# FOX attention of block 1 by pairs of heads: softmax normalised before the transposes, P V in feature order

## The chip, the cores and the metric

The kernel runs on one core of a Trainium2 chip. The metric is the device time of one execution in microseconds, from the median of several runs. The engines are PE (TensorE), DVE (VectorE), ACT (ScalarE), POOL (GpSimd) and SP (SyncE, which here only issues DMAs). Each takes its instructions strictly in the order in which they stand in its own program, and waits on semaphores of the others.

## The reference

Two transformer layers in float32 on 256 tokens with width 2048. The change lies in the first, a hybrid layer that puts 16 meta tokens ahead of the sequence:

```python
xn = _rms(h, n1)
proj = xn @ w_in
z_rwkv, z_fox, z_gate = jnp.split(proj, (RWKV_COLS, RWKV_COLS + FOX_COLS), axis=-1)
...
y_a = _rwkv7(z_rwkv, w0, w2, a0, a2, g2, k_k, k_a, r_k, gn_w, gn_b)
y_b = _fox(z_fox, q_g, k_g, f_bias)
...
merged = g_a * (y_a @ w_a) + g_b * (y_b @ w_b)
h = h + merged @ w_o
```

`_fox` is softmax attention with a forget gate over 16 heads of 64 features, in blocks of queries (the 16 meta queries' own outputs are dropped at the end):

```python
sc = jnp.einsum('bqhd,bkhd->bhqk', q[:, s:e], k[:, :e]).astype(F32) * ATTN_SCALE
sc = sc + c[:, :, s:e, None] - c[:, :, None, :e]
...
p = jax.nn.softmax(jnp.where(causal, sc, -jnp.inf), axis=-1)
outs.append(jnp.einsum('bhqk,bkhd->bqhd', p.astype(v.dtype), v[:, :, :e]))
```

`_rwkv7` is a linear recurrence over tokens with 16 heads of 64, followed by a group norm. A feed-forward layer, and a second layer with stick-breaking and latent attention, follow unchanged.

## The kernel before

Large products are made of three products of split operands (`mm3`): a weight tile comes by SP into one of three `raw` buffers, ACT casts it to `hi` (L219), DVE subtracts to get `lo` (L220), and PE multiplies hi by hi, hi by lo and lo by hi (all PE products are recorded at L240, the body of `mm`). Names in the profile are tile tags: `g`, `q` and `f` are PSUM banks (four, two and two of them): `g` for projections and gates, `q` for the RWKV work, `f` for FOX.

Block 1 goes through four groups q of four RWKV heads (`rwkv(q)`, a generator that yields between its stages) and four of four FOX heads (`fox(q)`). The loop interleaves them: projections and Gram matrices of RWKV group q, then the group norm of the group before, then the inverse and recurrence of group q, then `fox(q)`, then some of the eight gate products (`gate(n)`, weights w_g, results kept in DRAM as gdr).

One RWKV group is a long serial chain: the Gram matrices gt go through DRAM (hd) into tile hs (tag `hq`); DVE inverts 32x32 blocks by 31 steps of substitution (L573 multiplies, L576 adds; tiles xx and xt, tag `c`, xx loaded by POOL from xinit at L563); the result goes to DRAM (qd) and back (tags `hq` and `qf`); DVE copies and transposes it (L585, L587); small products complete the 64x64 inverses (q<-c,gt and q<-hq,c); a recurrence over five chunks follows (PE q<-sbd,x, DVE L633, PE q<-g_,qf, ACT L636, PE q<-uv,kb and q<-uv,gt, DVE L651); then a group norm (L664 to L679), and `to_units`, which transposes the result to feature order (four PE transposes, L420), copies it by ACT into `ysq` (L422) and writes it to DRAM (ydr0, L423).

A FOX head: POOL builds the bias (L738, L739), PE makes the scores for the two blocks of 128 queries (144 and 272 keys, contraction 64), DVE adds the bias and takes the maximum (L743), ACT exponentiates and sums (L745). PE transposes the unnormalised P: two transposes of the 16 meta keys (L748, L749) and three of 128 keys (L752 to L754). P V is a product with P's transposes as the stationary operand: five products of 64 columns into rows of queries. DVE divides by the sums (L764), and `to_units` transposes a group of four heads to feature order (through `ysf` into DRAM, ydr1).

After the loop the merge runs `for b in (1, 0)`: first y_b (read from ydr1) by w_b, 192 products, each half multiplied by its gate on DVE (L849), then y_a (read from ydr0, L836) by w_a, added to it. Then w_o. SP loads all weights in its own order, among them the reads of ydr.

The tile framework's scheduler sets the order of the instructions on each engine: from priorities, dependences, and the time at which a buffer of a tag's ring comes free. Weight loads are given priority (AHEAD = 300). `tmpf` takes a tile from a ring of five buffers with tag `c`; xx, xt, and most large temporaries of the RWKV group come from it. The group-norm, transposed and recurrent tiles therefore share buffers in the order in which they are made.

Of the kernel before, what the change touches and what calls it, by code (L numbers as in the profile page):

```python
# [17 lines left out]
META = 16  # L18
# [177 lines left out]
def body(tc, a, out):  # L196
# [5 lines left out]
    with ExitStack() as top:  # L202
# [83 lines left out]
        # ================= block 1: attention branches =================  # L286
        xh = T(xp, [128, 16, L], "X0", F32R)
        xl = T(xp, [128, 16, L], "X1", F32R)
        with ExitStack() as ph:
# [12 lines left out]

            def tmpp(shape):
                return T(rp, shape, "p", bufs=4)
# [76 lines left out]
            # forget gate: nc = cumsum(softplus(-(fl + bias)))  # L381
# [33 lines left out]
            def to_units(src, dst, tag):  # L415
                # src natural [128, 2, 256] -> dst [feature, 2, token]
                ps = bank(tag)
                for j in range(2):
                    for t in range(2):
                        P.transpose(ps[:, 256 * j + 128 * t:256 * j + 128 * t + 128], src[:, t, 128 * j:128 * j + 128], ident)  # L420
                ys = T(rp, [128, 512], "ys" + tag)
                S.copy(ys, ps)  # L422
                G.dma_start(dst, ys)  # L423

# [5 lines left out]
            def rwkv(q):  # L430
# [63 lines left out]
                # Gram matrices  # L494
# [25 lines left out]
                # bonus  # L520
# [6 lines left out]
                # natural v, and stacked [U | V]  # L527
# [17 lines left out]
                # natural [b | k]  # L545
# [14 lines left out]
                # inverse of (I - N): 32 x 32 diagonal blocks by substitution  # L560
# [36 lines left out]
                # L_ak V for every chunk  # L597
# [8 lines left out]
                # recurrence over chunks  # L606
# [50 lines left out]
                # group norm, bonus, gate  # L657
# [26 lines left out]
            def fox(q):  # L684
# [30 lines left out]
                vm = T(rp, [16, 256], "vm")  # L715
# [4 lines left out]
                S.copy(vn[:, :, :256], ps.rearrange("p (a b) -> p a b", b=256))  # L720
                ps = bank("f")
                for j in range(2):
                    P.transpose(ps[:16, 128 * j:128 * j + 128], vz[:, j, 0:META], ident)
                S.copy(vm, ps[:16, :256])
                yo = tmpo()
                st = T(rp, [128, 4, 8], "fst")
                for h in range(4):
                    j, er = h // 2, slice(64 * (h % 2), 64 * (h % 2) + 64)
                    hg = 4 * q + h
                    mb = tmpp([128, 416])  # L730
                    sm = tmpp([128, 416])
                    fm = C("fox")
                    rng = (slice(0, 144), slice(144, 416))
                    ps = bank("f")
                    for t in range(2):
                        n = 144 + 128 * t
                        m_ = mb[:, rng[t]]
                        G.tensor_scalar(out=m_, in0=ckb[:, h, :n], scalar1=cq[:, t, hg:hg + 1], scalar2=qs[:, 0, t, h:h + 1], op0=ALU.subtract, op1=ALU.mult)  # L738
                        G.tensor_tensor(out=m_[:, n - 128:], in0=m_[:, n - 128:], in1=fm, op=ALU.add)  # L739
                        mm(ps[:, rng[t]], qn[er, j, 128 * t:128 * t + 128], kn[er, j, :n])  # L740
                    for t in range(2):
                        sidx = 4 * t + h
                        V.tensor_tensor_reduce(out=sm[:, rng[t]], in0=ps[:, rng[t]], in1=mb[:, rng[t]], scale=1.0, scalar=-BIG, op0=ALU.add, op1=ALU.max, accum_out=st[:, 0, sidx:sidx + 1])  # L743
                        V.tensor_scalar(out=st[:, 1, sidx:sidx + 1], in0=st[:, 0, sidx:sidx + 1], scalar1=qs[:, 2, t, h:h + 1], scalar2=None, op0=ALU.mult)  # L744
                        S.activation(sm[:, rng[t]], sm[:, rng[t]], AF.Exp, bias=st[:, 1, sidx:sidx + 1], scale=qs[:, 1, t, h:h + 1], accum_out=st[:, 2, sidx:sidx + 1])  # L745
                    pt, pm = tmpp([128, 3, 128]), tmpp([16, 2, 128])
                    ps = bank("f")
                    P.transpose(ps[:16, 0:128], sm[:, 0:16], ident)  # L748
                    P.transpose(ps[:16, 128:256], sm[:, 144:160], ident)  # L749
                    V.tensor_copy(pm.rearrange("p a b -> p (a b)"), ps[:16, 0:256])  # L750
                    po = bank("f")
                    P.transpose(po[:, 0:128], sm[:, 16:144], ident)  # L752
                    P.transpose(po[:, 128:256], sm[:, 160:288], ident)
                    P.transpose(po[:, 256:384], sm[:, 288:416], ident)  # L754
                    S.copy(pt.rearrange("p a b -> p (a b)"), po[:, 0:384])
                    hs_ = slice(64 * h, 64 * h + 64)
                    for t in range(2):
                        o = po[:, 384 + 64 * t:448 + 64 * t]
                        mm(o, pm[:, t], vm[:, hs_], True, False)
                        mm(o, pt[:, t], vn[:, 0, hs_], False, t == 0)  # L760
                        if t:
                            mm(o, pt[:, 2], vn[:, 1, hs_], False, True)
# [420 lines left out]
```

## Time and profile before

| | |
|---|---|
| median of 3 runs | 2046.07 us (2041.98 to 2047.33) |
| profiled execution, its span | 2038.6 us |
| PE busy | 2010.6 us (99%) |
| DVE, ACT, POOL busy | 1219.6, 953.1, 160.4 us |
| mean DMA rate | 178 GB/s |
| idle stretches of PE over 2 us after the start | 172.6 (3.0 us) and 741.5 (2.5 us) |

The profiled execution is one run of its own; its time is given by the span, from its first to its last instruction. A row of the timeline gives the start, the duration, the engine, the line, the operation, the tile written <- the tiles read, the shape of the stationary operand for PE (rows*columns), the shapes and the count of the instructions that the row joins, and in brackets the idle time before and what ended it. A plain float32 product is recorded as two instructions.

### The profile page before, as it was taken

To read this page: it belongs to the slowest core of one execution; us is meant where nothing else is said; L and a number is where in the kernel's file an instruction comes from. 1 tells how busy PE (TensorE), PEld (TensorE's weight loads), DVE (VectorE), ACT (ScalarE), POOL (GpSimd) and SP (SyncE) were. 2 spreads that over 40 slices of the span, in tenths; PEclk is the share of its full clock that TensorE was granted. 3 is DMA by queue.
4 is the path that set the end of the run, shared out by engine and by line. 5 is a ranking of instruction groups with operands and counts; after the bars stand their busy time and mean duration, and the time that the engine had idled before them with its cause. 6 is when DMAs were issued, how large, how long until landed. Compare 5 with 4: busy or idle time off the path is not lost.

```text
span 2038.6 us, 29657 instructions
## 1 busy us (share of the span) xinstructions
PE 2010.6 (99%) x11510; PEld 1732.1 (85%) x11510; DVE 1219.6 (60%) x2117; ACT 953.1 (47%) x1266; POOL 160.4 (8%) x226
## 2 busy tenths in 40 slices
PE   7999999999999999999999999999999999999998
PEld 7998979989977778888888888888888889998886
DVE  7686675786774656555555554455555565666555
ACT  6544553555443434554444433444444555444443
POOL 4033131122121000000000000000000000000000
PEclk9999999999999999999999999999999999999999
DMA  5544455454455686555555566555555566444564
GB/s 192 178 147 119 144 162 166 132 168 144 146 155 174 204 285 234 187 186 193 187 191 188 188 196 192 193 193 186 187 192 188 175 207 191 145 136 155 185 193 142
DMA packets 118381, 363.19 MB, mean 178 GB/s; under 512 B 28353, under 2 KB 28641, under 8 KB 118241
## 3 DMA queue, kind: packets, MB, share of 16 engines
q1 hardware_dynamic: 113264, 344.97, 52.9%
q0 software_dynamic: 4976, 16.33, 2.6%
q8 instruction: 90, 1.47, 0.3%
q14 instruction: 51, 0.41, 0.1%
HBM read 351.65 MB, written 9.60 MB: 177 GB/s over the span
## 4 chain that ended last, share of the span: by engine, by line
PE 93%; DMA 3%; DVE 2%; ACT 1%; issue 0%; SPq 0%; POOL 0%; DVEq 0%; ACTq 0%
PE g L240 82%; PE q L240 4%; PE f L240 4%; DMA raw<-in_w_b 1%; DVE lo L220 1%; DMA raw<-in_w_A 1%; PE q L810 1%; PE f L810 1%; DMA hq<-qd 1%; ACT hi L219 0%; DMA x<-in_xT 0%; DMA ydr<-ysq 0%; DMA qd<-c 0%; DVE X L320 0%; DMA raw<-in_w_a 0%
## 5 line engine op out<-in xcount | busy, mean ns | idle before, releaser
L220 DVE TENSOR_TENSOR lo<-raw,hi 128x1024 fp32r<-128x1024 f32 (+2 forms) x633 | 775.7, 1226 | 613.3 <-ACT hi L219 608.0
L240 PE MATMUL g<-hi,X 128*128 128x512 f32 (+1 forms) x3344 | 1046.4, 392 | 3.3 <-issue 2.5
L219 ACT CAST hi<-raw 128x1024 fp32r<-128x1024 f32 (+2 forms) x633 | 661.5, 1045 | 821.7 <-PE g L240 697.0
L240 PEld LDWEIGHTS g<-hi,X 128*128 128x128 f32 x3344 | 628.1, 189 | 132.6 <-issue 4.7
L240 PE MATMUL g<-lo,X 128*128 128x512 f32 (+1 forms) x1672 | 656.5, 393 | 1.5 <-DVE lo L220 1.5
L240 PE MATMUL g<-X,hi 128*128 128x272 f32 (+4 forms) x2176 | 431.0, 293 | 9.4 <-ACT hi L219 5.9
L240 PEld LDWEIGHTS g<-lo,X 128*128 128x128 f32 x1672 | 315.6, 189 | 66.1 <-DVE lo L220 2.8
L240 PEld LDWEIGHTS g<-X,hi 128*128 128x128 f32 (+2 forms) x2176 | 345.4, 190 | 17.4 <-ACT hi L219 5.9
L240 PE MATMUL g<-X,lo 128*128 128x272 f32 (+3 forms) x1088 | 319.0, 293 | 0.1
L240 PEld LDWEIGHTS g<-X,lo 128*128 128x128 f32 (+1 forms) x1088 | 206.6, 190 | 2.8 <-issue 0.7
L240 PE MATMUL g<-hi,Y 128*128 128x512 f32 x544 | 170.8, 390 | 0.0
L240 PEld LDWEIGHTS g<-hi,Y 128*128 128x128 f32 x544 | 102.2, 188 | 20.7
L240 PE MATMUL g<-lo,Y 128*128 128x512 f32 x272 | 106.7, 392 | 0.0
L922 POOL DMA_DIRECT2D cst<-in_cst x1 | 0.5, 543 | 833.0 <-DMA raw<-in_w_cq 833.0
L240 PEld LDWEIGHTS g<-lo,Y 128*128 128x128 f32 x272 | 51.1, 188 | 10.3
L738 POOL TENSOR_SCALAR p<-ckb,cq,qs 128x144 f32<-128x144 f32 (+1 forms) x32 | 44.4, 1390 | 39.1 <-DVE fst L744 21.6
L573 DVE TENSOR_TENSOR c<-hq,c 108x42 f32<-108x42 f32 (+31 forms) x236 | 40.7, 205 | 2.8 <-DMA hq<-hd 2.7
L576 DVE TENSOR_TENSOR c<-c 108x42 f32<-108x42 f32 (+31 forms) x236 | 41.5, 207 | 0.3
L366 POOL TENSOR_TENSOR d<-z 128x272 f32<-128x272 f32 (+3 forms) x28 | 22.5, 806 | 128.5 <-DVE z L365 76.2
L745 ACT ACTIVATE p<-p,fst,qs 128x144 f32<-128x144 f32 (+1 forms) x32 | 17.7, 555 | 29.1 <-DVE fst L744 24.9
L739 POOL TENSOR_TENSOR p<-p,cst 128x128 f32<-128x128 f32 x32 | 23.3, 744 | 0.1
L628 POOL TENSOR_TENSOR sp<-sbd,pp 64x128 f32<-64x128 f32 x24 | 14.6, 610 | 83.8 <-DVE sbd L651 61.5
(449 smaller groups left out, 1426.7 us busy)
## 6 DMA issues: line engine op xcount, KB each, us to landing
raw<-in_w_gu SPq DMA_DIRECT2D x176, 512.0 KB
raw<-in_w_A SPq DMA_DIRECT2D x100, 512.0 KB
raw<-in_w_dn SPq DMA_DIRECT2D x88, 512.0 KB
raw<-in_w_g SPq DMA_DIRECT2D x64, 512.0 KB
raw<-in_w_o SPq DMA_DIRECT2D x32, 512.0 KB
raw<-in_w_qk SPq DMA_DIRECT2D x32, 512.0 KB
raw<-in_w_out SPq DMA_DIRECT2D x32, 512.0 KB
raw<-in_w_b SPq DMA_DIRECT2D x16, 512.0 KB
```

Of the source, the lines that this page charges most:

```text
L219: S.copy(hi, src)
L220: V.tensor_tensor(out=lo, in0=src, in1=hi.bitcast(F32), op=ALU.subtract)
L240: P.matmul(o, l, r, start=start, stop=stop, **k)
L366: G.tensor_tensor(out=d[:m, t1:], in0=z[:m, t1:L], in1=z[:m, 1 + t1:], op=ALU.subtract)
L573: V.tensor_tensor(out=t_, in0=hs[:108, j, j + 1:].unsqueeze(1).to_broadcast([108, k_, w]), in1=xs[:, :, j:j + 1].to_broadcast([108, k_, w] ...
L576: V.tensor_tensor(out=xs[:, :, j + 1:], in0=xs[:, :, j + 1:], in1=t_, op=ALU.add)
L628: G.tensor_tensor(out=sp[64 * e:64 * e + 64], in0=blk_(old, e), in1=dec(e), op=ALU.mult)
L738: G.tensor_scalar(out=m_, in0=ckb[:, h, :n], scalar1=cq[:, t, hg:hg + 1], scalar2=qs[:, 0, t, h:h + 1], op0=ALU.subtract, op1=ALU.mult)
L739: G.tensor_tensor(out=m_[:, n - 128:], in0=m_[:, n - 128:], in1=fm, op=ALU.add)
L745: S.activation(sm[:, rng[t]], sm[:, rng[t]], AF.Exp, bias=st[:, 1, sidx:sidx + 1], scale=qs[:, 1, t, h:h + 1], accum_out=st[:, 2, sidx:sid ...
L810: P.transpose(ps[:, o:o + 128], src[:, t, 128 * (k + j):128 * (k + j) + 128], ident)
L922: G.dma_start(cst2, a["cst2"])
```

## The change

- `to_units`: the tile that holds the transposed result, `ys`, comes from the ring of five (`tmpf`, tag `c`) and no longer has a buffer of its own. `to_units` now serves RWKV alone.
- FOX heads are taken by pairs. The bias is written into the tile of P itself. The scores of the pair go to two banks, with the two heads' operands in the two row halves of the array (partitions 0 to 63 and 64 to 127).
- P is normalised by DVE (two multiplications a head) ahead of its transposes; the division of the output goes.
- Meta keys: P is transposed 32 columns at a time, head 0 by a transpose, head 1 by a product with the identity into partitions 32 to 63 (the sixteen columns too many meet zeros). v of the meta keys is padded with zeros (`vpad`) to a block matrix `vd` of two heads.
- P V: now v is the stationary operand and P's transpose streams, 256 columns for both blocks of queries at once. The heads of a pair write the two halves of the output's partitions, so the output is in feature order; one ACT copy for a pair goes into `ysf`. The transposes to feature order go.

The lines behind `fox` move by 14 (L849 is now L863), those of `to_units` by -3 (L420 is now L417); those of `rwkv` keep their numbers.

```diff
@@ -299,9 +299,6 @@
-    def tmpp(shape):
-        return T(rp, shape, "p", bufs=4)
...
@@ -413,16 +410,19 @@
...
     def to_units(src, dst, tag):
         ps = bank(tag)
         for j in range(2):
             for t in range(2):
                 P.transpose(ps[:, 256 * j + 128 * t:256 * j + 128 * t + 128], src[:, t, 128 * j:128 * j + 128], ident)
-        ys = T(rp, [128, 512], "ys" + tag)
+        ys = tmpf([128, 512])
         S.copy(ys, ps)
         G.dma_start(dst, ys)
+    vpad = T(rp, [128, 2, 64], "vpad")
+    G.memset(vpad, 0.0)
...
@@ -712,59 +712,73 @@
         for j in range(2):
             V.tensor_tensor(out=vz[:, j], in0=next_a(), in1=rs, op=ALU.mult)
         vn = tmpo()
-        vm = T(rp, [16, 256], "vm")
+        vd = T(rp, [64, 256], "vm")
         ps = bank("f")
         for t in range(2):
             for j in range(2):
                 P.transpose(ps[:, 256 * t + 128 * j:256 * t + 128 * j + 128], vz[:, j, META + 128 * t:META + 128 * t + 128], ident)
         S.copy(vn[:, :, :256], ps.rearrange("p (a b) -> p a b", b=256))
+        for e in range(2):
+            V.tensor_copy(vpad[64 * e:64 * e + 64, :, 32 * e:32 * e + 16], vz[64 * e:64 * e + 64, :, 0:META])
         ps = bank("f")
         for j in range(2):
-            P.transpose(ps[:16, 128 * j:128 * j + 128], vz[:, j, 0:META], ident)
-        S.copy(vm, ps[:16, :256])
-        yo = tmpo()
+            P.transpose(ps[:64, 128 * j:128 * j + 128], vpad[:, j], ident)
+        S.copy(vd, ps[:64, :256])
+        ys = T(rp, [128, 512], "ysf")
         st = T(rp, [128, 4, 8], "fst")
-        for h in range(4):
-            j, er = h // 2, slice(64 * (h % 2), 64 * (h % 2) + 64)
-            hg = 4 * q + h
-            mb = tmpp([128, 416])
-            sm = tmpp([128, 416])
-            fm = C("fox")
-            rng = (slice(0, 144), slice(144, 416))
-            ps = bank("f")
+        fm = C("fox")
+        rng = (slice(0, 144), slice(144, 416))
+        for j in range(2):
+            sm = T(rp, [128, 2, 416], "p", bufs=2)
+            for e in range(2):
+                hg = 4 * q + 2 * j + e
+                for t in range(2):
+                    n = 144 + 128 * t
+                    m_ = sm[:, e, rng[t]]
+                    G.tensor_scalar(out=m_, in0=ckb[:, 2 * j + e, :n], scalar1=cq[:, t, hg:hg + 1], scalar2=qs[:, 0, t, 2 * j + e:2 * j + e + 1], op0=ALU.subtract, op1=ALU.mult)
+                    G.tensor_tensor(out=m_[:, n - 128:], in0=m_[:, n - 128:], in1=fm, op=ALU.add)
+            sc = [bank("f") for _ in range(2)]
             for t in range(2):
-                n = 144 + 128 * t
-                m_ = mb[:, rng[t]]
-                G.tensor_scalar(out=m_, in0=ckb[:, h, :n], scalar1=cq[:, t, hg:hg + 1], scalar2=qs[:, 0, t, h:h + 1], op0=ALU.subtract, op1=ALU.mult)
-                G.tensor_tensor(out=m_[:, n - 128:], in0=m_[:, n - 128:], in1=fm, op=ALU.add)
-                mm(ps[:, rng[t]], qn[er, j, 128 * t:128 * t + 128], kn[er, j, :n])
+                for e in range(2):
+                    er = slice(64 * e, 64 * e + 64)
+                    mm(sc[e][:, rng[t]], qn[er, j, 128 * t:128 * t + 128], kn[er, j, :144 + 128 * t])
+            for e in range(2):
+                h = 2 * j + e
+                for t in range(2):
+                    sidx = 4 * t + h
+                    m_ = sm[:, e, rng[t]]
+                    V.tensor_tensor_reduce(out=m_, in0=sc[e][:, rng[t]], in1=m_, scale=1.0, scalar=-BIG, op0=ALU.add, op1=ALU.max, accum_out=st[:, 0, sidx:sidx + 1])
+                    V.tensor_scalar(out=st[:, 1, sidx:sidx + 1], in0=st[:, 0, sidx:sidx + 1], scalar1=qs[:, 2, t, h:h + 1], scalar2=None, op0=ALU.mult)
+                    S.activation(m_, m_, AF.Exp, bias=st[:, 1, sidx:sidx + 1], scale=qs[:, 1, t, h:h + 1], accum_out=st[:, 2, sidx:sidx + 1])
+                V.reciprocal(st[:, 3, h:8:4], st[:, 2, h:8:4])
+                for t in range(2):
+                    V.tensor_scalar(out=sm[:, e, rng[t]], in0=sm[:, e, rng[t]], scalar1=st[:, 3, 4 * t + h:4 * t + h + 1], scalar2=None, op0=ALU.mult)
+            pm = T(rp, [64, 256], "pm")
+            pts = []
+            tp = [bank("f") for _ in range(2)]
             for t in range(2):
-                sidx = 4 * t + h
-                V.tensor_tensor_reduce(out=sm[:, rng[t]], in0=ps[:, rng[t]], in1=mb[:, rng[t]], scale=1.0, scalar=-BIG, op0=ALU.add, op1=ALU.max, accum_out=st[:, 0, sidx:sidx + 1])
-                V.tensor_scalar(out=st[:, 1, sidx:sidx + 1], in0=st[:, 0, sidx:sidx + 1], scalar1=qs[:, 2, t, h:h + 1], scalar2=None, op0=ALU.mult)
-                S.activation(sm[:, rng[t]], sm[:, rng[t]], AF.Exp, bias=st[:, 1, sidx:sidx + 1], scale=qs[:, 1, t, h:h + 1], accum_out=st[:, 2, sidx:sidx + 1])
-            pt, pm = tmpp([128, 3, 128]), tmpp([16, 2, 128])
-            ps = bank("f")
-            P.transpose(ps[:16, 0:128], sm[:, 0:16], ident)
-            P.transpose(ps[:16, 128:256], sm[:, 144:160], ident)
-            V.tensor_copy(pm.rearrange("p a b -> p (a b)"), ps[:16, 0:256])
-            po = bank("f")
-            P.transpose(po[:, 0:128], sm[:, 16:144], ident)
-            P.transpose(po[:, 128:256], sm[:, 160:288], ident)
-            P.transpose(po[:, 256:384], sm[:, 288:416], ident)
-            S.copy(pt.rearrange("p a b -> p (a b)"), po[:, 0:384])
-            hs_ = slice(64 * h, 64 * h + 64)
-            for t in range(2):
-                o = po[:, 384 + 64 * t:448 + 64 * t]
-                mm(o, pm[:, t], vm[:, hs_], True, False)
-                mm(o, pt[:, t], vn[:, 0, hs_], False, t == 0)
-                if t:
-                    mm(o, pt[:, 2], vn[:, 1, hs_], False, True)
-            V.reciprocal(st[:, 3, h:8:4], st[:, 2, h:8:4])
-            V.tensor_tensor(out=yo[:, :, hs_], in0=po[:, 384:512].rearrange("p (t v) -> p t v", v=64), in1=st[:, 3, h:8:4].unsqueeze(2).to_broadcast([128, 2, 64]), op=ALU.mult)
-        to_units(yo[:, :, :256], ydr[1][q], "f")
+                P.transpose(tp[t][:32, 384:512], sm[:, 0, 144 * t:144 * t + 32], ident)
+                mm(tp[t][32:64, 384:512], sm[:, 1, 144 * t:144 * t + 32], ident)
+                V.tensor_copy(pm[:, 128 * t:128 * t + 128], tp[t][:64, 384:512])
+            for e in range(2):
+                for k_, c0 in enumerate((16, 160, 288)):
+                    P.transpose(tp[e][:, 128 * k_:128 * k_ + 128], sm[:, e, c0:c0 + 128], ident)
+                pt = T(rp, [128, 384], "pt", bufs=2)
+                S.copy(pt, tp[e][:, :384])
+                pts.append(pt)
+            yb = bank("f")
+            mm(yb[:, :256], vd[:, 128 * j:128 * j + 128], pm, True, False, skip_group_check=True)
+            for e in range(2):
+                mm(yb[64 * e:64 * e + 64, :256], vn[:, 0, 128 * j + 64 * e:128 * j + 64 * e + 64], pts[e][:, 0:256], False, False, skip_group_check=True)
+            for e in range(2):
+                mm(yb[64 * e:64 * e + 64, 128:256], vn[:, 1, 128 * j + 64 * e:128 * j + 64 * e + 64], pts[e][:, 256:384], False, True, skip_group_check=True)
+            S.copy(ys[:, 256 * j:256 * j + 256], yb[:, :256])
+        G.dma_start(ydr[1][q], ys)
```

How the instructions stand on the engines, around the chain of RWKV group 3 (in these rows the numbers behind names tell tiles apart). First PE before: the last rows are FOX scores and P V, q<-c,gt is the product behind the inverse of group 3, and the g rows are gate products.

```order
L240 MATMUL f_6853<-f_6752,p_6847 128x64 x2
L240 MATMUL f_6867<-f_6346,f_6345 128x272
L240 MATMUL q_6161<-c_6159,gt_5901 32x32 x16
L240 MATMUL g_7085<-hi_7195,X1_79 128x512
L240 MATMUL g_7084<-hi_7213,X0_78 128x512
L240 MATMUL g_7084<-lo_7214,X0_78 128x512
L240 MATMUL g_7084<-hi_7213,X1_79 128x512
L240 MATMUL g_7085<-hi_7213,X0_78 128x512
L240 MATMUL g_7085<-lo_7214,X0_78 128x512
```

PE now, from the last w_b products (g<-hi,X1) to the beginning of the recurrence:

```order
L240 MATMUL g_7873<-hi_7929,X1_7626 128x512
L240 MATMUL g_7873<-lo_7930,X1_7626 128x512
L240 MATMUL g_7873<-hi_7929,X1_7626 128x512
L240 MATMUL q_6106<-c_6104,gt_5846 32x32 x16
L240 MATMUL q_6125<-hq_6098,c_6123 32x32 x16
L240 MATMUL q_6144<-uv_5906,gt_5846 64x64 x8
L240 MATMUL q_6154<-uv_5906,gt_5846 64x64 x8
L240 MATMUL q_6167<-uvm_5907,gtm_5847 32x64 x4
L240 MATMUL q_6166<-g__6165,hq_6098 32x64 x4
L240 MATMUL q_6178<-uvm_5907,kbm_5929 64x64 x4
L240 MATMUL q_6190<-sbd0_477,x4_5830 128x128 x2
```

PE now, from the recurrence's last chunk over the transposes of `to_units` (L417) to the first w_a products (g<-hi,X3):

```order
L240 MATMUL q_6271<-sbd1_478,x4_5830 128x128 x2
L240 MATMUL q_6270<-g__6269,qf_6100 64x64 x4
L240 MATMUL q_6271<-uv_5906,gt_5846 64x64 x4
L417 MATMUL q_6851<-ident_76,c_6164 128x128 x4
L240 MATMUL g_7958<-hi_7961,X3_7625 128x512
L240 MATMUL g_7959<-hi_7961,X3_7625 128x512
L240 MATMUL g_7958<-lo_7962,X3_7625 128x512
```

q<-c,gt of group 3 stood among FOX and gate products, with g products right behind it; now it stands behind the last w_b product, and no g product stands between it and the first w_a product (23 rows of PE).

DVE before, at the end of the inverse of group 3 (L573, L576) and at L585 and L587:

```order
L573 TENSOR_TENSOR c_6029<-hq_5943,c_6028 108x6
L220 TENSOR_TENSOR lo_7178<-raw_7176,hi_7177 128x1024
L576 TENSOR_TENSOR c_6028<-c_6028,c_6029 108x6
L763 RECIPROCAL fst_6765<-fst_6765 128x2
L220 TENSOR_TENSOR lo_7196<-raw_7194,hi_7195 128x1024
L750 COPY p_6848<-f_6849 16x256
L220 TENSOR_TENSOR lo_7214<-raw_7212,hi_7213 128x1024
L585 COPY qf_6155<-hq_6153 32x16x32
L587 STREAM_TRANSPOSE c_6159<-hq_6153 32x512
L220 TENSOR_TENSOR lo_7239<-raw_7237,hi_7238 128x1024
```

DVE now, at the place where the gate of w_b's last products is multiplied (L863):

```order
L573 TENSOR_TENSOR c_5974<-hq_5888,c_5973 108x42
L863 TENSOR_TENSOR X0_7627<-gate_7870,g_7872 128x512
L573 TENSOR_TENSOR c_5974<-hq_5888,c_5973 108x33
L576 TENSOR_TENSOR c_5973<-c_5973,c_5974 108x3x14
L863 TENSOR_TENSOR X0_7627<-gate_7870,g_7873 128x512
L576 TENSOR_TENSOR c_5973<-c_5973,c_5974 108x3x11
```

From there 47 instructions of L573 and L576 alone lead to this end:

```order
L576 TENSOR_TENSOR c_5973<-c_5973,c_5974 108x5x2
L573 TENSOR_TENSOR c_5974<-hq_5888,c_5973 108x6
L576 TENSOR_TENSOR c_5973<-c_5973,c_5974 108x6
L585 COPY qf_6100<-hq_6098 32x16x32
L587 STREAM_TRANSPOSE c_6104<-hq_6098 32x512
L596 COPY qf_6100<-q_6125 32x16x32
L619 COPY g__6165<-q_6167 32x256
```

Weight splits (L220) stood among the last inverse instructions and up to L585; now none does, and the multiplications by w_b's gate stand inside the inverse.

POOL before, around the load of xx for group 3 (c<-in_xinit) and the write of group 2's result (ydr0):

```order
L583 MEMSET qf_6155 32x16x32
L660 DMA c_6001<-in_gn 128x256 x2
L563 DMA c_6028<-in_xinit 128x352
L738 TENSOR_SCALAR p_6799<-ckb_6340,cq_264,qs_6347 128x144
L738 TENSOR_SCALAR p_6799<-ckb_6340,cq_264,qs_6347 128x272
L739 TENSOR_TENSOR p_6799<-p_6799,cst_86 128x128 x2
L423 DMA ydr0_473<-ysq_6025 128x512
L776 DMA gdr_479<-gate_7079 128x1024
```

POOL now, around the same:

```order
L790 DMA gdr_481<-gate_7609 128x1024
L855 DMA gate_7636<-gdr_481 128x1024
L855 DMA gate_7714<-gdr_481 128x1024
L855 DMA gate_7792<-gdr_481 128x1024
L563 DMA c_5973<-in_xinit 128x352
L420 DMA ydr0_473<-c_5970 128x512
L855 DMA gate_7870<-gdr_481 128x1024
L855 DMA gate_7956<-gdr_481 128x1024
```

The load of xx stood among the FOX biases (L738), ahead of the gates' writes (L776) and reads (L841); now it stands behind all writes of the gates (gdr<-gate) and three of their reads, right ahead of the write of ydr0 of group 2.

## The prediction

> **What bounds the kernel now.** I read the shares by engine, then the chain that ended last, then the windows by stage, and last the timelines around the two places where TensorE stands still.
>
> ```profile
> PE 2010.6 (99%) x11510; PEld 1732.1 (85%) x11510; DVE 1219.6 (60%) x2117; ACT 953.1 (47%) x1266; POOL 160.4 (8%) x226
> ...
> PE 93%; DMA 3%; DVE 2%; ACT 1%; issue 0%; SPq 0%; POOL 0%; DVEq 0%; ACTq 0%
> ```
>
> TensorE is busy for all but 28 us of a span of 2038.6 us, and the chain runs on it for 93%. So PE work taken away comes off the time one for one, and so does any place where PE runs dry.
>
> ```profile
> 172.00:182.00 10.00, 6.84 (x59) 6.23 (x58) 4.91 (x15) 2.81 (x6) 2.18 (x3) 0.66 0.48 134
> ...
> 700.00:760.00 60.00, 55.99 (x233) 44.68 (x232) 36.53 (x41) 26.82 (x27) 2.67 (x5) 0.94 0.81 274
> ```
>
> The columns are the stretch, its length, busy time of PE, PEld, DVE, ACT and POOL with counts, the granted clock, DMA share and GB/s. Two short stretches are not full: the first inverse (172 to 182) and the merge (700 to 760, 4.0 us idle, and 6% of 60 us = 3.6 us lost to the clock).
>
> ```profile
> 175.65 1.91 PE L240 MATMUL q<-c,gt 32*32 32x32 f32 x32 [3.01 <-DVE c L587]
> ...
> 603.69 1.24 PE L240 MATMUL q<-c,gt 32*32 32x32 f32 x32
> ```
>
> The first row is the product that follows the inverse of RWKV group 0: PE stood 3.0 us for DVE's transpose. The second is the same product in group 3: no idle time before it, because projection products stood ahead of it on PE. The whole forecast rests on this: the inverse, its trip through DRAM and the recurrence are a serial chain that costs nothing as long as PE has other products between its links.
>
> **The change, part 1: the FOX heads.** Per head, before:
>
> ```profile
> 151.59 0.27 PE L748 MATMUL f<-ident,p 128*16 128x128 f32 x1
> ...
> 151.73 0.37 PE L240 MATMUL g<-X,hi 128*128 128x258 f32 x1
> ...
> 152.16 0.27 PE L749 MATMUL f<-ident,p 128*16 128x128 f32 x1
> ...
> 152.41 0.36 PE L240 MATMUL g<-X,hi 128*128 128x258 f32 x1
> ...
> 155.70 0.51 PE L240 MATMUL f<-f 64*128 64x144 f32 x2
> 156.13 0.43 PE L240 MATMUL f<-vm,p 16*128 16x64 f32 x2
> ...
> 157.81 0.72 PE L240 MATMUL f<-f 64*128 64x272 f32 x2
> 158.46 0.51 PE L240 MATMUL g<-X,hi 128*128 128x258 f32 x2
> ```
>
> From start to start: transposes 0.14 + 0.25 = 0.39, scores and P V 158.46 - 155.70 = 2.76. That is 3.15 for a head, 50.4 for 16, and about 1.6 for the 16 transposes to feature order (L420) that go: 52.
>
> After, per pair: two scores of 144 columns (0.43 each, 155.70 to 156.13) and two of 272 (0.65, 157.81 to 158.46) are 2.16 one after the other, 1.08 if the array halves run together. Whether halves run together is seen in the recurrence:
>
> ```profile
> 651.27 0.45 PE L240 MATMUL q<-uv,kb 128*64 128x64 f32 x8
> 651.56 0.63 PE L240 MATMUL q<-uv,gt 128*64 128x64 f32 x8
> 652.12 0.50 PE L240 MATMUL g<-lo,X 128*128 128x512 f32 x1
> ```
>
> Both have eight records of 64 columns; the first alternates column halves and takes 0.29, the second stays in one and takes 0.56. The order puts the scores of the two heads alternately in only 3 of the 8 pairs, so I take 1.08 x 3 + 2.16 x 5 = 14.0 for all. Transposes: six of 128 columns at 0.07 (three and two in the rows above take about that each), two of 32 columns at no more than 0.11, and two plain products with the identity.
>
> ```profile
> 1739.71 0.39 PE L240 MATMUL f<-kr,qr 128*128 128x128 f32 x2
> 1739.93 0.60 PE L240 MATMUL f<-X 128*128 128x256 f32 x2
> 1740.37 0.59 PE L240 MATMUL f<-kr,qr 128*128 128x256 f32 x2
> ```
>
> A plain float32 product of 128 columns takes 0.22 and one of 256 takes 0.44 (start to start). So transposes are 0.42 + 0.22 + 0.44 = 1.08 for a pair. P V: three of 256 columns and two of 128 are 1.76 one by one, 1.1 with the column halves together. All eight pairs: 14.0 + 8.6 + 8.8 = 31.4 with the halves together, 36.7 without, or 40 with the scores serial too. The saving is 52 less that: 20.6, or 12 where no halves run together. Against it, every pair goes from the full array to row halves, to column halves and back. The 64-row scores above show what leaving the full array may cost: 144 columns at the 0.44 for 256 would be 0.25, and they take 0.43, 0.18 more. Three such changes a pair are 24 x 0.18 = 4.3, which leaves 16, or 8 where no halves run together; I take **-14**, nearer the first, since the rows at 651 show halves that do. Ends: -5 (five changes a pair, 7.2, off the 12) and -21 (none).
>
> [...]
>
> DVE work: 16 divisions of 128x128 and 16 copies of 16x256 go, 32 normalising passes, 16 copies of 64x128 and 8 of vpad come, 24 short passes more, on an engine that is 60% busy. Cover: PE's projections. In group 0, where DVE sets the end of the 3.0 us stall, PE arrives earlier by its own saving, about 5 us, and DVE's row of work ahead of L587 is about as much changed; I leave that stall as it is, with 3 to 6 us in the range. POOL's and ACT's counts are the same within 4, hidden.
>
> **Part 2: the tile `ys` in to_units.** It moves from its own buffer into the ring of five (`tmpf`) from which the next inverse takes xx and xt. The edit itself costs nothing. But xx's load from xinit for group 3, on POOL, now stands right ahead of group 2's write of ydr0 and behind all the gates; before, it stood ahead of the gates too. With it the whole chain of group 3 comes to stand behind all 192 w_b products, with nothing on PE between its links, from q<-c,gt to the transposes of to_units. On DVE the two multiplications of the last w_b products by their gate (L849 before, L863 now) stand 47 inverse instructions ahead of L585. And ydr0, which the chain ends in, is what w_a's products read, so they can't fill. All of the chain from the last w_b product on is then PE's:
>
> ```profile
> 730.73 1.28 DVE L849 TENSOR_TENSOR X<-gate,g 128x512 f32<-128x512 f32 x2
> ...
> 132.28 0.28 DVE L573 TENSOR_TENSOR c<-hq,c 108x26 f32<-108x26 f32 x2
> 132.51 0.28 DVE L576 TENSOR_TENSOR c<-c 108x26 f32<-108x26 f32 x2
> ...
> 162.68 0.17 DVE L576 TENSOR_TENSOR c<-c 108x6 f32<-108x6 f32 x1
> ...
> 174.56 0.41 DVE L585 COPY qf<-hq 32x512 f32<-32x512 f32 x1 [7.51 <-DMA hq<-qd]
> ...
> 454.16 0.17 DVE L576 TENSOR_TENSOR c<-c 108x6 f32<-108x6 f32 x1
> ...
> 462.38 0.41 DVE L585 COPY qf<-hq 32x512 f32<-32x512 f32 x1 [1.92 <-DMA hq<-qd]
> ...
> 657.10 0.60 PE L240 MATMUL q<-sbd,x 128*128 128x128 f32 x4
> ...
> 657.75 0.42 DVE L633 TENSOR_TENSOR g__6268<-q,x 64x256 f32<-64x256 f32 x1 [0.69 <-PE q L240]
> ...
> 662.71 0.67 PE L240 MATMUL q<-g__6268,qf 64*64 64x64 f32 x8
> ...
> 663.42 0.37 ACT L636 COPY uv<-q 64x256 f32<-64x256 f32 x1 [1.65 <-PE q L240]
> ...
> 668.37 0.45 PE L240 MATMUL q<-uv,kb 128*64 128x64 f32 x8
> ...
> 669.31 0.99 DVE L651 SCALAR_TENSOR_TENSOR sbd<-q,pp,sp 64x64 f32<-64x64 f32 x4
> ```
>
> (a) The two multiplications 1.3. (b) 47 inverse instructions at 0.23 for two (132.28 to 132.51) 5.2. (c) From the last inverse instruction to L585, out to DRAM and back: 174.56 - 162.85 = 11.7, or 462.38 - 454.33 = 8.1; I take 9, nearer the latter since the queue is emptier at that point. (d) L585 to the product: 175.65 - 174.56 = 1.1. (e) The recurrence, five chunks, each a round of PE 0.65, DVE 0.42, PE 0.71, ACT 0.37, PE 0.94, DVE 0.99 = 4.1 from row to row; five less the last update, 19.4; ahead of them three small products and their copies, 3 x 1.24 + 2 x 0.41 = 4.6; together 24. 12 of these are PE's own, work that is there before too. After 15 us of idle PE will start slowly: the product took 1.91 after 3.0 us idle against 1.24 at full clock, with 0.66 granted. By that ratio 12 becomes 18, so (e) is **30**, ends 24 and 36.
>
> [...]
>
> ```profile
> L666 DVE TENSOR_TENSOR c<-c,st 128x512 f32<-128x512 f32 x4 | 2.8, 694 | 0.1
> ...
> L669 ACT ACT_TABLE_LOAD x2 | 2.6, 1283 | 0.0
> ...
> ydr<-ysq POOLq DMA_DIRECT2D x4, 256.0 KB, 3.8
> ...
> 738.94 4.19 SPq L235 DMA_DIRECT2D raw<-in_w_a  x3
> ...
> 744.03 0.70 PE L240 MATMUL g<-hi,X 128*128 128x512 f32 x2 [2.50 <-issue]
> ```
>
> (f) Group norm: eight full passes on DVE at about 0.69 = 5.5, one on ACT and three small ones 1.3, hand-overs 0.4, a table load 1.3 in half the cases: 8.5, ends 7.2 and 9. (g) Transposes and their copy 1.3. (h) The write of ydr0 4 (3.8 above). (i) SP's second read of ydr0 waits for that write, and w_a's loads are queued behind it: from the issue of w_a to its first product 744.03 - 738.94 = 5.1, and the read's own issue ahead of it, 6 together, ends 5 and 7. (The two w_o tiles that SP loads ahead of the read are wanted later; hidden.) (j) Restart at the low clock 2, ends 0 and 4. Sum: 1.3 + 5.2 + 9 + 1.1 + 30 + 8.5 + 1.3 + 4 + 6 + 2 = 68.4; less 12 of PE's own work **+56.4**, ends 45 and 69 from the ends of the terms. Given back: the 4.0 + 3.6 us of 700 to 760, whose waits for w_a fall into the new one: **-7.5**, ends 0 and -7.5.
>
> **Sum.** 2038.6 - 14 + 56.4 - 7.5 = 2073.5 for the profiled execution. The median of the runs shown, 2046.07, is 7.5 above that span, which I add: **2081 us**, 35 above before.
>
> **Rivals.**
>
> Covered tail (other side). If PE still has products to do while the chain runs, nothing of the 56 is seen and the saving stays, with half of what is given back: 2046 - 14 - 4 = 2028. For it speaks group 3 before, which ran without a gap (603.69). Against it the order on PE: the chain's products stand behind the last w_b product and ahead of the first w_a product. It decides at an exposed tail of 21.5 us (14 + 7.5): the trip (c) and (f) to (i) alone, 9 + 8.5 + 1.3 + 4 + 6 = 29, are over that.
>
> Shorter tail. All terms at their low ends and the whole saving of 21: 45 - 21 - 7.5 = +16.5, 2062; with (b) hidden as well, because w_b ends later than DVE's inverse, 2057.
>
> Longer tail. PE slow throughout, the trip 11.7, a long refill, halves serial and nothing given back: 69 - 5 = +64, 2110.
>
> Halves that do not run together. The saving is 5 to 8 instead of 14: 2087 to 2090, inside the range.
>
> The first stall grows. The 3.0 us at group 0 take in PE's saving there and DVE's new passes, 3 to 6 more: 2084 to 2087, inside the range.
>
> **How the numbers follow.** Forecast 0.78 (2060 to 2106, the two rivals inside the range included), longer 0.07, covered 0.06, shorter tail 0.09: 0.06 of it between 2052 and 2060, and 0.03 where a part of the recurrence is covered too and the exposed tail comes near the 21.5 us. 0.3%, 6 us, is about what a measurement of this kernel tells from no change. So faster 0.06, same 0.03, slower 0.06 + 0.78 + 0.07 = 0.91.
>
> **What would show it.** Right: one stretch of some 60 us, between the last w_b and the first w_a product, with PE busy for about a quarter of it and its clock under 0.7; q<-c,gt of group 3 waiting over 10 us for DVE's transpose at L587; w_a's first product waiting for lo; FOX heads at about (52 - 14) / 8 = 4.8 us of PE a pair. Wrong: g products between the recurrence's, or a busy PE in that stretch; then the time is below 2046. A pair at 5.9 us, (52 - 5) / 8, would say that mode changes took the saving.

## The result and the profile after

The changed kernel takes 2075.57 us (median of 4 runs, 2071.73 to 2078.29) against 2046.70 before (4 runs): a ratio of 1.0141, 95% interval 1.0121 to 1.0161, so 29 us slower. The forecast was 2081, the range 2060 to 2106. The two profiled executions lie further apart, 2038.6 and 2076.5 us of span: executions of one kernel differ, and the mean clock granted to PE differs with them (of the runs of before beside the bank experiments one took 2038.41 us at 0.995, another 2052.30 at 0.988), and the profiled one of before was a quick one, at 0.994.

First the page's own lines of the changed kernel (busy by engine, then the chain that ended last by engine), and of the windows by stage the rows around the merge:

```profile
PE 2004.4 (97%) x11430; PEld 1722.7 (83%) x11430; DVE 1215.6 (59%) x2141; ACT 955.1 (46%) x1272; POOL 157.0 (8%) x227
...
PE 88%; issue 1%; ACT 1%; DMA 1%; DVE 1%; SPq 0%; POOL 0%; DVEq 0%; ACTq 0%; POOLq 0%
```

```profile
690.00:770.00 80.00, 48.72 (x332) 40.85 (x330) 38.93 (x165) 12.77 (x21) 6.16 (x13) 0.66 0.23 67
712.00:728.00 16.00, 0.89 (x7) 0.46 (x6) 8.26 (x54) 0.00 (x0) 0.54 (x1) 0.63 0.25 56
728.00:761.00 33.00, 25.02 (x224) 21.46 (x223) 6.64 (x21) 4.30 (x10) 3.47 (x8) 0.50 0.04 9
782.00:789.00 7.00, 6.22 (x16) 4.49 (x17) 4.31 (x4) 2.88 (x4) 0.00 (x0) 0.57 0.88 276
```

PE's share falls from 99 to 97%, and nearly all of it in one place: of 44 us more idle time 40 lie between 700 and 800 us. From 712.8 to 727.9 us PE does nothing; then it is busy for three quarters of 33 us, but at half the clock (0.50), and with small products. The last row is the restart.

The timeline of the changed kernel there, PE first and then DVE, at the links of group 3's chain:

```profile
712.40 0.39 PE L240 MATMUL g<-hi,X 128*128 128x512 f32 x1
727.89 1.88 PE L240 MATMUL q<-c,gt 32*32 32x32 f32 x32 [15.11 <-DVE c L587]
...
759.90 1.11 PE L240 MATMUL q<-uv,gt 128*64 128x64 f32 x8 [0.46 <-ACT uv L636]
769.20 1.08 PE L417 MATMUL q<-ident,c 128*128 128x128 f32 x4 [8.18 <-DVE c L679]
782.75 1.19 PE L240 MATMUL g<-hi,X 128*128 128x512 f32 x2 [12.47 <-DMA raw<-in_w_o]
```

```profile
719.30 0.17 DVE L576 TENSOR_TENSOR c<-c 108x6 f32<-108x6 f32 x1
726.71 0.42 DVE L585 COPY qf<-hq 32x512 f32<-32x512 f32 x1 [7.24 <-DMA hq<-qd]
...
761.45 0.69 DVE L664 TENSOR_REDUCE st<-c 128x8 f32<-128x512 f32 x1 [3.17 <-ACT c L655]
...
768.36 0.69 DVE L679 TENSOR_TENSOR c<-c,gq 128x512 f32<-128x512 f32 x1
```

The last w_b product (712.40) is followed by the whole chain: the rest of the inverse to 719.5, the trip through DRAM to 726.7, the recurrence from 727.9 to 761.0, the group norm to 769.1, the transposes, and w_a's first product at 782.75. That is 70.0 us from 712.8, and the same product that followed without a gap at 603.69 before now waits 15.1 us. The name behind 782.75 (raw<-in_w_o) is only the last semaphore; the products needed ydr0, which was written from 771.2 on, and the w_a tile loaded behind its read.

Around it the two profiles balance. Before, w_a's first product came at 744.03 and 1294.6 us followed; now it comes at 782.75 and 1293.8 us follow. The 38 us between the two executions all lie ahead of w_a.

The FOX heads did get cheaper. Summed from each record's start to the next one's, scores, transposes of P (before, of the output too) and P V took 49.3 us of PE before and 34.1 now.

### The profile page after: what moved, and what is told of

Its sections match the earlier page's. It is cut to its first block, busy times and chain, and to the rows that moved or that the text cites. A ratio compares the mean times of both kernels' runs of the same rounds, so it can differ in the third digit from the quotient of the medians.

```text
span 2076.5 us, 29561 instructions
## 1 busy us (share of the span) xinstructions
PE 2004.4 (97%) x11430; PEld 1722.7 (83%) x11430; DVE 1215.6 (59%) x2141; ACT 955.1 (46%) x1272; POOL 157.0 (8%) x227
## 4 chain that ended last, share of the span: by engine, by line
PE 88%; issue 1%; ACT 1%; DMA 1%; DVE 1%; SPq 0%; POOL 0%; DVEq 0%; ACTq 0%; POOLq 0%
PE g L240 79%; PE q L240 4%; PE f L240 3%; PE q L824 1%; PE f L824 1%; ACT hi L219 0%; DMA raw<-in_w_b 0%; DMA raw<-in_w_o 0%; PE f L768 0%; ACT L472 0%; DVE c L573 0%; DVE c L576 0%; DMA hq<-qd 0%; PE f L1077 0%; PE q L1077 0%
## 5 line engine op out<-in xcount | busy, mean ns | idle before, releaser
L220 DVE TENSOR_TENSOR lo<-raw,hi 128x1024 fp32r<-128x1024 f32 (+2 forms) x633 | 776.0, 1226 | 638.2 <-ACT hi L219 635.4
L240 PE MATMUL g<-X,hi 128*128 128x272 f32 (+4 forms) x2176 | 425.4, 292 | 9.1 <-ACT hi L219 6.8
L573 DVE TENSOR_TENSOR c<-hq,c 108x42 f32<-108x42 f32 (+31 forms) x236 | 37.6, 194 | 6.2 <-DMA hq<-hd 5.2
L576 DVE TENSOR_TENSOR c<-c 108x42 f32<-108x42 f32 (+31 forms) x236 | 39.9, 203 | 0.3
L754 ACT ACTIVATE p<-p,fst,qs 128x144 f32<-128x144 f32 (+1 forms) x32 | 17.7, 554 | 12.9 <-DVE fst L753 12.8
L240 PE MATMUL q<-uv,gt 64*64 64x64 f32 (+1 forms) x256 | 22.5, 245 | 0.5 <-ACT uv L636 0.5
L240 PEld LDWEIGHTS q<-uv,gt 64*64 64x64 f32 (+1 forms) x256 | 19.9, 158 | 2.4 <-issue 0.9
```

The lines of the kernel that those rows point to most:

```text
L220: V.tensor_tensor(out=lo, in0=src, in1=hi.bitcast(F32), op=ALU.subtract)
L240: P.matmul(o, l, r, start=start, stop=stop, **k)
L573: V.tensor_tensor(out=t_, in0=hs[:108, j, j + 1:].unsqueeze(1).to_broadcast([108, k_, w]), in1=xs[:, :, j:j + 1].to_broadcast([108, k_, w] ...
L576: V.tensor_tensor(out=xs[:, :, j + 1:], in0=xs[:, :, j + 1:], in1=t_, op=ALU.add)
L754: S.activation(m_, m_, AF.Exp, bias=st[:, 1, sidx:sidx + 1], scale=qs[:, 1, t, h:h + 1], accum_out=st[:, 2, sidx:sidx + 1])
```

## The experiments

**Where the tail comes from.** Theory R: the tile `ys`, taken from the ring of five, moves the chain. Theory F: the FOX rewrite does. One line of the changed kernel goes back:

```diff
-                ys = tmpf([128, 512])
+                ys = T(rp, [128, 512], "ysf")
```

> The changed kernel with one line back: the transposed result of to_units has a buffer of its own again (shared with FOX's output tile). Theory R (the tile in the ring moves RWKV group 3's chain behind all w_b products): the 70 us between the last w_b and the first w_a product are filled with gate products again, and FOX's saving of 15 us on PE stays: 2031 us (2022 to 2038). Theory F (the FOX rewrite itself, its later P and its changes of array halves, delays the chain): 2065 us or more.

Measured: 2046.58 us (before on the same chip 2044.33), ratio 1.0012, interval 1.0003 to 1.0021. Neither theory had it. Theory R was right that most of the tail goes, some 26 us by the two ratios (1.0141 and 1.0012); but FOX's 15 us don't show against the kernel before. The timeline shows two stretches that stayed:

```profile
742.12 1.09 PE L417 MATMUL q<-ident,c 128*128 128x128 f32 x4 [8.39 <-DVE c L679]
756.25 1.19 PE L240 MATMUL g<-hi,X 128*128 128x512 f32 x2 [13.04 <-ACT hi L219]
```

The inverse and the recurrence have gate and w_b products between their links again, but the group norm, the transposes and the way of ydr0 through DRAM still stand behind the last w_b product: 21.4 us of idle PE.

The other half of the test is the kernel before with that one line of the change, and FOX heads untouched:

```diff
-                ys = T(rp, [128, 512], "ys" + tag)
+                ys = tmpf([128, 512]) if tag == "q" else T(rp, [128, 512], "ys" + tag)
```

> The kernel before with that one line of the change: only the RWKV result of to_units comes from the ring of five; FOX heads as before. Theory R: the tail appears without any FOX change, with nothing saved: 2046.7 + 44 = 2091 us (2080 to 2105), and an idle stretch of 12 us or more ahead of q<-c,gt of group 3. Theory F: no change, 2047 us.

Measured: 2082.67 us, ratio 1.0184 (1.0167 to 1.0200). The line alone costs 38 us, and no FOX change is needed for it. The expectation was 8 us too high, and its idle stretch ahead of q<-c,gt is 2.8 us, not 12:

```profile
733.35 1.17 PE L240 MATMUL q<-c,gt 32*32 32x32 f32 x32 [2.80 <-DVE c L587]
...
774.15 1.09 PE L420 MATMUL q<-ident,c 128*128 128x128 f32 x4 [8.40 <-DVE c L679]
788.00 1.19 PE L240 MATMUL g<-hi,X 128*128 128x512 f32 x2 [12.75 <-DMA raw<-in_w_o]
```

Here w_b's products end at 730.6, 18 us later than in the changed kernel, so the inverse and its trip run beside them; from q<-c,gt to w_a's first product it is the same, 55 us in both.

**Why one buffer moves a chain.** Theory N: five buffers are too few when `ys` takes one. Theory O: the buffers of a ring are handed out in the order in which the code first writes the tiles, so the next inverse's tiles wait for the group norm's end. A ring of six (FOX's output tile was halved to make room) tells them apart, and then a ring of six in which xx and xt are taken and first written ahead of the group norm:

```diff
-                return T(rp, shape, "c", bufs=5)
+                return T(rp, shape, "c", bufs=6)
...
-                yield
-
                 xx = tmpf([128, 11, 32])
                 xt = tmpf([128, 352])
                 G.dma_start(xx, a["xinit"])
+                G.memset(xt, 0.0)
+                yield
+
```

(The first hunk is ring_of_six, both are six_early; the halving of FOX's output tile, in both runs, is left out here.)

> The changed kernel with a ring of six buffers instead of five (FOX's output tile is halved and written to DRAM by pairs to make room). Theory N (five buffers are too few): the tail goes, 2031 us. Theory O (the ring's buffers are handed out in the order in which the code first writes the tiles, so the next inverse's tiles wait for the end of the group norm however many buffers there are): as the changed kernel, 2075 us (2066 to 2084).

> As ring_of_six, and the two tiles of the next inverse are taken, and first written, ahead of the group norm of the group before in the code; the result of to_units stays in the ring. Theory O: the tail goes, 2032 us (2023 to 2042). If any tile of to_units in the ring does harm, whatever the order: 2075 us.

Measured: ring_of_six 2075.00 us, ratio 1.0152 (1.0136 to 1.0168), the same as the changed kernel (1.0141), with the same 15.1 us of idle PE ahead of q<-c,gt: theory N falls. six_early 2038.45, ratio 0.9973 (0.9961 to 0.9985): the ring is harmless once the order of taking is turned round, as theory O says, at 6 us over what it expected. It keeps the same two stretches as own_buffer:

```profile
729.82 1.09 PE L417 MATMUL q<-ident,c 128*128 128x128 f32 x4 [8.39 <-DVE c L680]
743.69 1.19 PE L240 MATMUL g<-hi,X 128*128 128x512 f32 x2 [12.78 <-ACT hi L219]
```

**Where FOX's 15 us went.** Theory C: into that exposed end of the chain. The kernel's eight PSUM banks are split 4 for projections, 2 for RWKV, 2 for FOX. With a third bank for the RWKV products, the scheduler's order has the transposes of group 3 ahead of the last w_b product again. The edit is one line on top of own_buffer, and the same line alone on the kernel before:

```diff
-BANKS = {"g": 4, "q": 2, "f": 2}
+BANKS = {"g": 3, "q": 3, "f": 2}
```

> As own_buffer, with the PSUM banks split 3 for projections, 3 for the RWKV products, 2 for FOX (4, 2, 2 before). In its order the transposes of to_units for group 3 stand 79 rows of PE ahead of the last w_b product again, and not behind it as in own_buffer. Theory C (what eats FOX's 15 us in own_buffer is the exposed end of the chain: 8.4 + 13.0 us idle, and the restart): 2046.6 - 22 = 2025 us (2018 to 2036), with no idle stretch over 4 us near the merge. Theory G (PE needs four projection banks): idle time before g products after 760 us, 2046 us or more.

> The kernel before with the same split of banks and nothing else. It has no exposed end of the chain, so theory C: 2044 us (2036 to 2048), at most the 3 us stall of group 0 and the 4 us of the merge to gain. Theory G: 2050 us or more. Against it banks_3_3_2 shows what the FOX rewrite is worth where nothing of the chain is exposed: 15 us of PE work less by the traces.

Measured: banks_3_3_2 2024.21 us, ratio 0.9900 (0.9880 to 0.9920), and before with the same split 2043.92, ratio 0.9999 (0.9982 to 1.0015). So the split is worth nothing by itself, and between these two, where no chain is exposed, the FOX rewrite is worth 20 us by the medians. PE's records show 16 (49.3 before, 33.3 in banks_3_3_2), and the 4 us between lie within the two intervals. What is left near the merge is 2.8 us ahead of w_a, as before (2.5), and 2.5 us ahead of q<-c,gt of group 3:

```profile
605.33 1.28 PE L240 MATMUL q<-c,gt 32*32 32x32 f32 x32 [2.47 <-DVE c L587]
...
733.13 1.19 PE L240 MATMUL g<-hi,X 128*128 128x512 f32 x2 [2.83 <-issue]
```

Then the changed kernel itself, `ys` in the ring, with that split:

> The changed kernel as it is (result of to_units in the ring of five) with the banks split 3, 3, 2. Its order puts g products between the links of group 3's recurrence again, but the transposes of to_units still behind the last w_b product. Theory C: only the end of the chain is exposed, group norm, write and read of ydr0, restart, as in own_buffer: 2024 + 22 = 2046 us (2038 to 2054), with idle stretches of 8 and 13 us. If the ring itself costs time whatever stands on PE: 2065 us or more; if three RWKV banks cure it: 2024 us.

Measured: 2039.55 us, ratio 0.9952 (0.9928 to 0.9976); 6 us under the expectation's middle, inside its range. The two stretches are there about as expected (5.9 and 12.9 us), the others not. By the ratios (0.9952, and 0.9900 for banks_3_3_2) the tile in the ring still costs 0.5%, some 11 us, with three RWKV banks:

```profile
731.50 1.12 PE L417 MATMUL q<-ident,c 128*128 128x128 f32 x4 [5.95 <-DVE c L679]
745.53 1.19 PE L240 MATMUL g<-hi,X 128*128 128x512 f32 x2 [12.91 <-ACT hi L219]
```

How late the chain runs is seen at one instruction, DVE's transpose at L587, in its first and last start (groups 0 and 3): before, the changed kernel, own_buffer and banks_3_3_2, in this order.

```profile
L587 DVE STREAM_TRANSPOSE c<-hq x4: 692/692/693, 174.9 to 602.4; 32x512 f32<-32x512 f32 x4
```

```profile
L587 DVE STREAM_TRANSPOSE c<-hq x4: 692/692/693, 182.1 to 727.1; 32x512 f32<-32x512 f32 x4
```

```profile
L587 DVE STREAM_TRANSPOSE c<-hq x4: 692/692/693, 182.1 to 649.9; 32x512 f32<-32x512 f32 x4
```

```profile
L587 DVE STREAM_TRANSPOSE c<-hq x4: 692/693/693, 178.0 to 604.6; 32x512 f32<-32x512 f32 x4
```

A group takes 142 us before ((602.4 - 174.9) / 3), 182 in the changed kernel, 156 with a buffer for `ys`, 142 with that and a third RWKV bank. Why the chain needs 156 with two banks beside the new FOX heads, which touch none of these banks, is open: no run took the FOX steps apart for it.

**The halves of the array.** The forecast counted on the heads of a pair running at the same time in different halves. This kernel is banks_3_3_2 with each pair's products issued head by head:

```diff
-                    for t in range(2):
-                        for e in range(2):
+                    for e in range(2):
+                        for t in range(2):
                             er = slice(64 * e, 64 * e + 64)
...
-                    for e in range(2):
                         mm(yb[64 * e:64 * e + 64, 128:256], vn[:, 1, ...], pts[e][:, 256:384], False, True, ...)
```

> As banks_3_3_2, with the products of a FOX pair issued head by head (scores of head 0, then of head 1; both P V products of head 0, then of head 1), so that neighbours on PE seldom lie in different halves. If halves run at the same time (start to start 121 ns a record for 256 columns in the changed kernel, against some 220 by themselves): P V 7.1 to 14 us, scores 11.6 to 15 us, together 7 to 10 us slower than banks_3_3_2. If the order doesn't matter: within 3 us of it.

Measured: 2023.86 us, ratio 0.9895 (0.9876 to 0.9915) to before: the same as banks_3_3_2. The expectation failed, but not because halves do not overlap. P V of one pair, banks_3_3_2 and then halves_serial:

```profile
176.86 0.87 PE L240 MATMUL f<-pt,f 128*64 128x256 f32 x8
177.66 0.52 PE L240 MATMUL f<-tw,hi 96*128 96x272 f32 x2
```

```profile
175.34 0.88 PE L240 MATMUL f<-pt,f 128*64 128x256 f32 x8
176.15 0.52 PE L240 MATMUL f<-tw,hi 96*128 96x272 f32 x2
```

Two products of 256 columns and two of 128 take 0.80 and 0.81 us from start to start; one after the other they would take 2 x 0.44 + 2 x 0.22 = 1.32 by the rows that the prediction shows. Head by head, both products of the first head stand ahead of the second head's first in the order: if that one had started no earlier than they, the pair would have taken some 0.44 + 0.44 + 0.22 = 1.10 (an estimate from the same rows), and it took 0.81. So the edit took the halves apart in the order and not in time, and its run can't price them; the records do.

The row halves show the same. In the changed kernel the scores of two heads that stand together, and then those of one head alone, take 0.91 and 0.89 us (each row joins the products of 144 and of 272 columns):

```profile
133.66 0.97 PE L240 MATMUL f<-f 64*128 64x144 f32 x8
134.57 0.39 PE L240 MATMUL g<-X,hi 128*128 128x272 f32 x1
...
161.19 0.97 PE L240 MATMUL f<-f 64*128 64x144 f32 x4
162.08 0.39 PE L240 MATMUL g<-X,lo 128*128 128x258 f32 x1
```

The second head costs next to nothing (0.02 us) when it stands beside the first. In five of the eight pairs the order keeps the two apart, and an estimate of what that costs is 5 x 0.9 = 4.5 us.

**The clock in the tail.** The changed kernel with 66 products more, which fill the idle 15 us:

```diff
+                if b:
+                    dps = bank("g")
+                    for i_ in range(66):
+                        mm(dps, u_[:, 0, i_ % 8, 0:128], u_[:, 1, 2 * (i_ % 4):2 * (i_ % 4) + 2].rearrange("p a b -> p (a b)"))
```

> The changed kernel with 66 products more of 512 columns, whose results nobody reads, on PE between the last w_b product and q<-c,gt of group 3: they fill the 15 us in which PE waits for the inverse and its trip. If the low clock of the tail comes from that idle time and work at half load keeps a high clock: recurrence (33 us) at full clock, 26 us, and 2068 us in all (2064 to 2071). If the clock falls again in the half busy recurrence: 2073 us or more, the same as the changed kernel.

Measured: 2075.60 us, ratio 1.0148 (1.0122 to 1.0173); the same as the changed kernel, the second of the two expected outcomes. PE was kept busy for 14 of the 15 us, and the clock fell all the same:

```profile
710.88 13.76 PE L240 MATMUL g<-X 128*128 128x512 f32 x60
726.01 1.17 PE L240 MATMUL q<-c,gt 32*32 32x32 f32 x32 [1.37 <-DVE c L587]
727.84 1.91 PE L240 MATMUL q<-hq,c 32*32 32x32 f32 x32 [0.67 <-ACT c L592]
```

```profile
714.00:730.00 16.00, 13.96 (x114) 11.65 (x114) 3.74 (x23) 0.58 (x1) 0.00 (x0) 0.91 0.22 52
730.00:735.00 5.00, 4.40 (x41) 4.08 (x40) 0.88 (x2) 1.16 (x2) 0.00 (x0) 0.50 0.00 0
735.00:760.00 25.00, 16.69 (x120) 13.64 (x120) 6.63 (x22) 2.94 (x8) 3.46 (x8) 0.50 0.05 11
```

The first small product takes 1.17 us, the second, with as many records of the same shape, 1.91, and from 730 to 760 us the granted clock is 0.50 throughout.

## Why the prediction was right

**The mechanism.** The chain of group 3 stands behind all w_b products, with nothing between its links: read from the order, and shown by the row at 727.89 and by before_ring. Most of the signs came: one stretch (70.0 us for "some 60"), the wait of over 10 us for L587 (15.1), the clock under 0.7 (0.50 in the recurrence), a pair of FOX heads at 4.3 us for 4.8. Two did not. PE was to be busy "for about a quarter of it", and was for 25 us of the recurrence's 33 alone. And w_a's first product was to wait for lo; the profile names a DMA, and the product reads hi, whose cast on ACT ended at 782.65.

**The terms of the tail**, forecast and measured: (a) and (b), multiplications and inverse, 6.5 and 6.7 (712.8 to 719.5); (c) the trip 9 and 7.2; (d) 1.1 and 1.2; (e) the recurrence 30 and 33.6 (727.89 to 761.45); (f) the group norm 8.5 and 7.6 (761.45 to 769.05, without a table load); (g) to (i), transposes, write, read and w_a, 11.3 and 13.7 (769.05 to 782.75); (j) restart 2, an estimate that no row shows, and 3.0 (7 us at 0.57). Sum 68.4 and 73.0. Two are off by more than 2 us, (g) to (i) and (e), whose 30 makes 18 of PE's own 12 us, by the 1.91 and 1.24 of before. Its upper end, 36, takes them twice, as at a clock of 0.50, and 0.50 is what the window from 728 to 761 shows: the 36 is 2.4 above what was measured, the 30 is 3.6 below. The prediction laid the slow recurrence to the 15 us of idle ahead of it. That idle was not needed: with 14 us of it filled, in warm_tail, the recurrence ran at the same 0.50.

**The FOX saving.** Forecast 14, measured 49.3 - 34.1 = 15.2 by the records' starts. Its parts are less near than their difference, which is luck in part: before, 52 was counted and 49.3 measured; after, 38 (31.4 and some 6.6 for changes of mode, the author's estimate, which no run shows apart) and 34.1. Scores took 11.6 for 14.0, since one head's take 0.9 and not 1.08; transposes 10.5 for 8.6; P V 12.0 for 8.8 with the halves together (14.1 one by one), the excess mostly at its first product (0.61 a pair for 0.44) and its last two (0.41 for 0.22). A 64-row product right behind whole-array ones is dear here: the 256 columns of f<-pm,vm take 0.62 (159.76 to 160.38 below) where 0.44 is the price in the whole array; no run separates the change of mode from what such a product costs by itself.

**The first stall.** The 3.0 us ahead of q<-c,gt of group 0 went, but in their place PE of the changed kernel waits as long, 30 us earlier, for P to be normalised (DVE L757), which now stands ahead of the transposes; the prediction had looked for that stall in the old place.

```profile
144.31 0.37 PE L763 MATMUL f<-ident,p 128*32 128x128 f32 x1 [3.54 <-DVE p L757]
...
159.76 0.70 PE L240 MATMUL f<-pm,vm 64*128 64x256 f32 x2
160.38 0.87 PE L240 MATMUL f<-pt,f 128*64 128x256 f32 x8
```

**The sum.** 73.0 less 12 (PE's own work, as forecast) and 15.2 is 45.8, and the spans differ by 37.9: 7.9 came back elsewhere, forecast 7.5. For the profiled execution the forecast was 2073.5, and its span is 2076.5. That the median came at 2075.6 and not at 2081 lies in the last step: the prediction added the 7.5 us between the profiled execution of before and its median, but that of the changed kernel, 2078.29, is 2.7 above the median (and 1.8 above its span). So the forecast was 3.0 too low for the span and 8.4 too high in the step to the median; that it came within 5.4 us is luck in part.

**The rivals.** The covered tail is not what happened, but its price was sound: with the chain covered the same FOX heads take 2024, forecast 2028. Halves do run together (0.80 us for the P V of a pair in banks_3_3_2, where its four products come to 1.32 one by one).

## What to carry to other kernels

A tile that moves into a shared ring adds no instruction, and cost 38 us here: where a scheduler hands out a ring's buffers in the order of the code, a late tile of one stage holds back the first tile of the next. Look at what stands between the links of the longest serial chain, in the order, and at what work is left for the bottleneck engine when the chain ends; a sixth buffer did not help, taking the tile from elsewhere or taking the next stage's tiles first did. A saving on the bottleneck engine (15 us here) is only seen if the chain beside it gets shorter too, or stays covered.

## What the runs showed of the hardware

- PE's clock fell without idle time just before it. In the kernel before, PE was busy for all of the 4.8 us from 600.0 to 604.8, with q<-c,gt of group 3 (603.69) directly behind other products, and the next 3.3 us were at half clock:

```profile
604.80:608.10 3.30, 3.30 (x11) 2.56 (x9) 0.86 (x6) 2.61 (x6) 0.00 (x0) 0.50 0.51 159
```

  In warm_tail 13.8 us of products without a gap (710.88), 1.4 us ahead of the same product, did not prevent it. Through the recurrence of the changed kernel, in which PE was busy for 25 of 33 us with small products, the clock stayed at 0.50; what in it kept the clock down is open, since no run varied one thing alone.
- Two heads' products in the two column halves overlap even when each half's products stand together in the order: 0.81 us for the pair in halves_serial, where the estimates are 1.32 one after the other and 1.10 with starts in the order. By these PE's products do not always start in the order of its program, other than the first section says.
- In the changed kernel two heads' scores in the two row halves take 0.91 us when they stand together (133.66), and one head's take 0.89 (161.19).
